# Big split products, term by term over the PSUM banks

## The chip, the cores and the metric

The kernel runs on one core of a Trainium2 chip. The metric is the device time of one execution in microseconds. A time is the median of several runs; beside it stands one execution recorded by the profiler, whose span is a little shorter than the runs' time.

## The reference, cut to what matters

One layer of a hybrid backbone: four token mixers (convolution module, mLSTM, gated DeltaNet, RWKV-7) on one combined input projection of 512 tokens (256 context, 256 latent), a gated merge, an output projection, and a gated ConvFFN on the 256 latent tokens.

```python
D_MODEL, SEQ, CTX_LEN, D_FF = 2048, 256, 256, 5632
sc, sx = split_cols(hc @ p['w_in']), split_cols(hx @ p['w_in'])      # all branches' columns
...                                                                  # scans of the branches
br = jnp.einsum('btnw,nwd->btnd', ys, w_br)
gates = jax.nn.sigmoid(gate_cols.reshape(*gate_cols.shape[:2], N_BRANCH, -1))
mx = jnp.sum(gates * br, axis=2) @ w_out
x = x + gt1x * rms_norm(mx, norm_g[l, 1])
...
u, v = jnp.split(h @ up, 2, axis=-1)
fx = (jax.nn.gelu(dwconv2d_grid(u, dw), approximate=True) * v) @ down
x = x + gt2x * rms_norm(fx, norm_g[l, 3])
```

Everything is float32.

## The kernel before, in words

**Split products.** A float32 product is made of three products in the faster fp32r type. Each operand is split in two parts: hi is the value rounded to fp32r, lo is what is left. The sum of hi·hi, hi·lo and lo·hi is the product. The activations' parts are `uh` and `ul` (in the FFN `u2h`, `u2l`, and `hh`, `hl` for the down product); a weight tile's parts are `hi` and `lo`. So each pair of a weight tile and an activation tile costs three matmuls, here called terms; one of the three needs the weight's `lo`.

**The weight stream.** A step handles 256 rows of a weight matrix, that is two K tiles of 128, for up to 512 columns. `load_split` (line 181) issues the DMA from SyncE into `raw`, lets ScalarE copy it into `hi` (line 192) and VectorE, or at times GpSimdE, subtract `hi` from `raw` into `lo` (line 194). `raw` has four buffers (five in the FFN), `hi` and `lo` two each (four in the FFN). A buffer is used again when its last reader is done: `raw` after the `lo` split, `hi` and `lo` after the last matmul that reads them.

**mode_b** (line 201, with `mode_b_steps`) keeps the weights stationary: out[channel, token], one PSUM bank per block of 128 channels, and up to four blocks in a set. A set has `nkt/2` steps, eight for the 2048 rows. It is used for most columns of the input projection and for FFN up.

**mode_a** (line 220) keeps the activations stationary: out[token, channel], one bank per tile of 128 tokens, 512 channels. It is used for the branch gates (16 sets of eight steps), for the merge (`merge`, 16 sets of two steps), for mLSTM's v and for the output projection. With `apart`, the last so many steps of a set are held back and done token tile by token tile; the output projection's last set does that with three steps.

In both, a step goes bank by bank: all six matmuls of one bank (two K tiles, three terms), then the next bank. The second term of mode_a and the third of mode_b needs `lo`.

**FFN down** (in `ffn`, line 1407) has 44 steps, one per K tile of 128 rows, 24 matmuls each, into eight banks: two token tiles `i` by two halves `q` by two quarters `r`. `load_split_row` (line 1515; `hi` at 1523, `lo` at 1524) loads each half of a step. The last three steps are held and go bank by bank.

**What sets the order.** The program's text gives the order of priority; the framework's scheduler (`schedule_with_timeline_sim=True`) then writes each engine's queue with a simulated timeline, and may draw an instruction ahead of another that it takes to be late. Matmuls into the same bank stay in order. On the chip each engine works its queue from front to back. The sets of columns run beside the branches' scans, so split work and scan work share VectorE and ScalarE. All matmuls are recorded at line 79, the helper `mm`.

Of the kernel before, what the change touches and what calls it, by code (L numbers as in the profile page):

```python
# [20 lines left out]
P = 128  # L21
D = 2048
# [10 lines left out]
# columns of the per-channel parameters: first one, number  # L33
# [8 lines left out]
class Kern:  # L42
# [4 lines left out]
    # ---------------------------------------------------------------- helpers  # L47
# [13 lines left out]
    def aux(self, name="aux", tag="aux"):  # L61
        """PSUM bank; its tag's banks go round in program order."""
        bufs = self.auxn.get(tag)
        assert bufs, tag
        return self.auxp.tile([P, 512], F32, tag=tag, name=name, bufs=bufs)
# [8 lines left out]
    def evp(self, name):  # L74
        """PSUM behind column sets and adaLN, apart from the recurrences'."""
        return self.wap.tile([P, 512], F32, tag="wa", name=name)
# [4 lines left out]
    def tr(self, out, in_, b=0):  # L81
        """out = in_.T; in_ starts at partition b."""
        k = in_.shape[0]
        self.nc.tensor.transpose(out, in_, self.ident[b : b + k, b : b + k])
# [9 lines left out]
    def rsqrt(self, pool, x, shape, tag):  # L94
        """x ** -0.5 in place of a small fp32 tile of positive values (Newton from a bit-level guess)."""
# [6 lines left out]
        # y (15 - 10 a + 3 a^2) / 3 of a = x y^2, then y' (3 - 9/64 x y'^2) 3/16  # L102
# [9 lines left out]
    # ---------------------------------------------------------------- constants  # L112
    def constants(self):
# [15 lines left out]
        # LM[:, kind, col] over (row % 64): 0 col>row, 1 col>=row, 2 col<row, 3 col<=row  # L129
# [7 lines left out]
        # block-diagonal 128x128 versions  # L137
# [19 lines left out]
    def first_params(self):  # L157
        """Per-channel parameters, one column per 128 channels; c and c_ctx first."""
# [5 lines left out]
    def params(self):  # L164
        nc, PC = self.nc, self.PC
        # a = 1 - mu0 - mu1 of the token shift
# [10 lines left out]
    # ---------------------------------------------------------------- weight stream  # L177
# [3 lines left out]
    def load_split(self, parts, width, rings=None):  # L181
        """parts: [(dram [256, w], column offset)] -> hi, lo tiles [128, 2, 512] in fp32r."""
# [13 lines left out]

    def mode_b(self, *a):
        for _ in self.mode_b_steps(*a):
            pass

    def mode_b_steps(self, parts_of, width, blocks, uh, ul, nkt, bank=None):
        """Weights stationary: out[channel, token]. blocks: (offset, M, token0, N, evacuate).
        One step per pair of K tiles; the evacuations follow the last."""
        ps = [bank("psB") if bank else self.mmp.tile([P, 512], F32, tag="mm", name="psB") for _ in blocks]
        n2 = nkt // 2
        for kg in range(n2):
            hi, lo = self.load_split(parts_of(kg), width)
            for bi, (off, M, t0, N, _) in enumerate(blocks):
                for k in range(2):
                    kt = 2 * kg + k  # L210
                    for j, (w, u) in enumerate(((hi, uh), (hi, ul), (lo, uh))):
                        self.mm(ps[bi][:M, :N], w[:, k, off : off + M], u[:, kt, t0 : t0 + N],
                                start=(kt == 0 and j == 0), stop=(kt == nkt - 1 and j == 2))
# [6 lines left out]
    def mode_a(self, parts_of, uh, ul, nkt, toks, evac, apart=0, rings=None):  # L220
        """Activations stationary: out[token, channel] for 512 channels. apart: this many last steps go by token tile."""
# [3 lines left out]
        for kg in range(n2):  # L225
            hl = self.load_split(parts_of(kg), 512, rings if kg % 2 else None)
            todo = [(kg, hl, ti) for ti in range(len(toks))]
            if kg >= n2 - apart:
                held.append(todo)
                todo = [t[ti] for ti in range(len(toks)) for t in held] if kg == n2 - 1 else []  # L230
            for g, (hi, lo), ti in todo:
                t0 = toks[ti]
                for k in range(2):
                    kt = 2 * g + k
                    for j, (u, w) in enumerate(((uh, hi), (uh, lo), (ul, hi))):
                        self.mm(ps[ti], u[:, kt, t0 : t0 + P], w[:, k, :],
                                start=(kt == 0 and j == 0), stop=(kt == nkt - 1 and j == 2))
# [3 lines left out]
    # ---------------------------------------------------------------- adaLN  # L241
    def wmod_steps(self, cb, dst, raws=None, gain=None):
        """One step per 256 rows of w_mod[:, 512 cb:][:512]; the last one leaves silu(c) @ it + b_mod in dst, feature-major
        [128, 4, 1 or 2]. The partial sums of column half h lie on rows 64 h + 32 k + {0: c, 1: c_ctx}."""
# [18 lines left out]
        if gain is not None:  # L263
            # a gate vector on every partition, times the norm's gain
# [25 lines left out]
    def mod_feed(self):  # L290
        """Steps of the other four adaLN vectors of the latent stream, taken beside the column sets: shift and scale of the
        FFN feature-major, the gates token-major."""
# [6 lines left out]
    def feed(self, upto=0):  # L299
        """As many adaLN steps as the rate says, and all before step `upto`."""  # L300
# [5 lines left out]
    # ---------------------------------------------------------------- phase 0  # L306
    def phase0(self, first, opened):
        """adaLN shift and scale of the mixer, modulated input u (context tokens first); `first`: the steps of
        column sets that run as its K tiles appear; `opened`: called before their last ones."""
# [38 lines left out]
        # what is left of u takes the place of the token tiles  # L348
# [42 lines left out]
    # ---------------------------------------------------------------- inverse of unit triangular 64x64 blocks  # L391
# [7 lines left out]
    def tinv(self, pool, tag, d, n, N, U, pool_rec=False, ptag="aux"):  # L399
        """U[:, j] = (I - N[:, j])^-1 for n matrices per half of the partitions: rows s on partitions (two blocks  # L400
# [1268 lines left out]
```

## Time and profile before

| | us |
|---|---|
| median of 3 runs | 2360.63 |
| lowest, highest | 2359.28, 2361.23 |
| profiled execution, span | 2358.9 |
| TensorE matmuls busy | 2250.4 (95%) |
| VectorE busy | 1478.0 (63%) |
| ScalarE busy | 987.1 (42%) |
| GpSimdE busy | 500.8 (21%) |

The profiled execution's own time is known by its span alone. The rows name engines PE (TensorE matmuls), PEld (its weight loads), DVE (VectorE), ACT (ScalarE), POOL (GpSimdE) and SP (SyncE, which issues the DMAs). A row of a group gives busy time, the mean duration of one in ns, and the idle time of the engine ahead of it with what ended it. A row of the timeline gives start, duration, engine, line, operation, out<-in and, in brackets, the idle time ahead. Matmuls are pipelined: a row's duration overlaps the next, and the pace is the distance of starts. `psB`, `psA` and `psD` are the banks of mode_b, mode_a and FFN down. In rows of windows the columns are length, then busy time and count for PE, PEld, DVE, ACT and POOL, then the granted clock of TensorE, the DMA engines' busy share and GB/s.

In time, the input's modulation lies from 0 to 150 us, the column sets and the scans to about 900, the gates' sets with scans beside them to about 1400, the merge and output projection to about 1560, FFN up from 1575 to 2106, and FFN down to the end.

### The profile page before, as it was taken

The numbers are of one execution on the slowest core, as the hardware profiler recorded it, in microseconds if no ns is written. First come the engines' busy times: TensorE is split into PE (matmuls) and PEld (weight loads), VectorE is DVE, ScalarE is ACT, GpSimd is POOL, SyncE is SP. The second block draws the span as 40 slices with busy tenths as digits, with TensorE's granted clock in tenths as the row PEclk, the third lists the DMA queues.
The fourth block names the chain that finished last, engine by engine and source line by source line (L and its number), as shares of the span: only waits on it lengthen the run. The fifth ranks groups of instructions, "written<-read, shape, count | busy, mean of one in ns | idle before, by whom it ended". The sixth has DMA issues, their size and how long they took to land.

```text
span 2358.9 us, 42865 instructions
## 1 busy us (share of the span) xinstructions
PE 2250.4 (95%) x16820; PEld 1846.2 (78%) x16820; DVE 1478.0 (63%) x3079; ACT 987.1 (42%) x1491; POOL 500.8 (21%) x849
## 2 busy tenths in 40 slices
PE   6979899999999899999999999989999999999998
PEld 3657677877888666767777777779999999998886
DVE  3357866643555976566556478566777677775554
ACT  4225644433444343233225544444444344444443
POOL 0012563533452995000001034010000000000000
PEclk8989899899999999999999999989999999999999
DMA  9934654454666677677668667567767666666563
GB/s 367 347 113 129 180 166 117 133 169 135 184 180 197 184 239 216 208 238 233 189 206 275 185 223 262 184 224 216 225 210 218 208 182 187 180 199 204 193 195 101
DMA packets 273612, 471.97 MB, mean 200 GB/s; under 512 B 41505, under 2 KB 80673, under 8 KB 272417
## 3 DMA queue, kind: packets, MB, share of 16 engines
q1 hardware_dynamic: 273122, 467.14, 63.6%
q8 instruction: 132, 2.16, 0.4%
q10 hardware_dynamic: 288, 2.10, 0.2%
q14 instruction: 70, 0.57, 0.1%
HBM read 440.33 MB, written 28.84 MB: 199 GB/s over the span
## 4 chain that ended last, share of the span: by engine, by line
PE 80%; DVE 8%; DMA 5%; ACT 2%; POOL 2%; issue 2%; SPq 0%; DVEq 0%; ACTq 0%; POOLq 0%
PE psB L79 35%; PE psA L79 20%; PE psD L79 10%; PE psw L79 4%; DVE lo L194 2%; DMA wraw<-in_w_mod 2%; PE psG L79 1%; DMA raw<-in_w_mix 1%; DVE cacc L858 1%; POOL riU L397 1%; PE pVN L79 1%; PE pKS L79 1%; PE pSn L79 1%; ACT hi L192 1%; PE psf L79 1%
## 5 line engine op out<-in xcount | busy, mean ns | idle before, releaser
L194 DVE TENSOR_TENSOR lo<-raw,hi 128x1024 fp32r<-128x1024 f32 (+2 forms) x485 | 603.6, 1246 | 449.7 <-ACT hi L192 440.2
L192 ACT ACTIVATE hi<-raw 128x1024 fp32r<-128x1024 f32 (+2 forms) x488 | 508.4, 1043 | 845.4 <-PE psB L79 383.7
L79 PE MATMUL psB<-u2h,lo 128*128 128x256 f32 x1408 | 396.7, 283 | 0.0
L79 PE MATMUL psB<-u2l,hi 128*128 128x256 f32 x1408 | 396.5, 283 | 0.2 <-DVE u2l L1354 0.2
L79 PE MATMUL psB<-u2h,hi 128*128 128x256 f32 x1408 | 395.5, 285 | 1.1 <-DVE u2h L1353 1.1
L79 PE MATMUL psA<-lo,uh 128*128 128x512 f32 x832 | 336.3, 405 | 12.6 <-DVE lo L194 12.3
L79 PE MATMUL psA<-hi,ul 128*128 128x512 f32 x832 | 329.8, 397 | 0.0
L79 PE MATMUL psA<-hi,uh 128*128 128x512 f32 x832 | 310.0, 404 | 2.2 <-ACT hi L192 2.2
L79 PE MATMUL psB<-uh,hi 128*128 128x256 f32 (+1 forms) x832 | 281.5, 347 | 24.4 <-ACT hi L192 17.8
L79 PE MATMUL psB<-ul,hi 128*128 128x256 f32 (+2 forms) x832 | 278.9, 340 | 0.0
L79 PEld LDWEIGHTS psB<-u2h,hi 128*128 128x128 f32 x1408 | 267.6, 192 | 10.8 <-issue 9.5
L79 PEld LDWEIGHTS psB<-u2l,hi 128*128 128x128 f32 x1408 | 269.9, 192 | 0.5 <-DVE u2l L1354 0.5
L79 PEld LDWEIGHTS psB<-u2h,lo 128*128 128x128 f32 x1408 | 269.8, 192 | 0.1
L79 PE MATMUL psB<-uh,lo 128*128 128x256 f32 (+2 forms) x832 | 263.1, 342 | 6.8 <-DVE lo L194 6.8
L79 PEld LDWEIGHTS psA<-lo,uh 128*128 128x128 f32 x832 | 156.9, 189 | 63.0 <-DVE lo L194 21.7
L79 PEld LDWEIGHTS psB<-uh,hi 128*128 128x128 f32 x832 | 159.9, 193 | 54.8 <-ACT hi L192 20.7
L79 PEld LDWEIGHTS psA<-hi,uh 128*128 128x128 f32 x832 | 153.5, 189 | 51.5 <-issue 15.0
L79 PEld LDWEIGHTS psA<-hi,ul 128*128 128x128 f32 x832 | 157.0, 189 | 33.6 <-issue 1.0
L79 PEld LDWEIGHTS psB<-uh,lo 128*128 128x128 f32 (+1 forms) x832 | 153.8, 192 | 32.3 <-DVE lo L194 9.6
L79 PEld LDWEIGHTS psB<-ul,hi 128*128 128x128 f32 (+1 forms) x832 | 160.6, 193 | 22.0 <-issue 6.1
L1524 DVE TENSOR_TENSOR lo<-raw,hi 128x1024 fp32r<-128x1024 f32 x88 | 107.6, 1225 | 78.3 <-ACT hi L1523 78.2
L1444 DVE SCALAR_TENSOR_TENSOR facc<-fpad,ffdw,facc 128x256 f32<-128x256 f32 x352 | 152.9, 488 | 0.2
(569 smaller groups left out, 3129.1 us busy)
## 6 DMA issues: line engine op xcount, KB each, us to landing
raw<-in_w_in SPq DMA_DIRECT2D x208, 512.0 KB, 4.5
raw<-in_ffn_up SPq DMA_DIRECT2D x176, 512.0 KB, 3.9
wraw<-in_w_mod SPq DMA_DIRECT2D x160, 512.0 KB, 5.3
raw<-in_ffn_down SPq DMA_DIRECT2D x88, 512.0 KB, 4.6
raw<-in_w_br SPq DMA_DIRECT2D x32, 512.0 KB, 4.8
raw<-in_w_out SPq DMA_DIRECT2D x32, 512.0 KB, 4.7
raw<-in_w_mod SPq DMA_DIRECT2D x32, 512.0 KB, 4.0
raw<-in_w_in SPq DMA_DIRECT2D x48, 256.0 KB, 3.7
```

Source lines behind the costliest of these rows:

```text
L79: self.nc.tensor.matmul(out, lhsT, rhs, start=start, stop=stop)
L192: nc.scalar.activation(hi[s], raw[s], AF.Copy)
L194: (nc.gpsimd if self.pool_lo >= 0 else nc.vector).tensor_tensor(lo[s], raw[s], hi[s].bitcast(F32), ALU.subtract)
L397: eng.tensor_tensor(U16[:, :, t], U16[:, :, t], m[:, :, t], ALU.add)
L858: nc.vector.scalar_tensor_tensor(a, cpad[:, i, t : t + 256], w(i, t), a, ALU.mult, ALU.add)
L1444: nc.vector.scalar_tensor_tensor(s3(acc), pad[:, dy : dy + 4, dx : dx + 64], tap(t, b), s3(acc), ALU.mult, ALU.add)
L1524: nc.vector.tensor_tensor(f(lo), f(raw), f(hi).bitcast(F32), ALU.subtract)
```

## The change

A new helper gives the order of a step's matmuls, as (bank, K tile, term). In the middle steps of a set, all but the first and the last, it goes term by term: for each term both K tiles, and for each of these all banks. In other steps it stays bank by bank. In mode_a the terms change places, so that the one with `lo` is the last everywhere; in mode_b it was the last already. Steps that `apart` holds back count as last ones, so they stay bank by bank. FFN down goes term by term over all eight banks in its first 41 steps, and bank by bank in the three held ones, with the term of `lo` last in both. The sets of the merge have two steps, so there only the order of terms changes. The numbers of instructions, tiles and buffers stay.

```diff
+    def turns(n, by_term):
+        if by_term:
+            return [(b, k, j) for j in range(3) for k in range(2) for b in range(n)]
+        return [(b, k, j) for b in range(n) for k in range(2) for j in range(3)]
...
     def mode_b_steps(self, parts_of, width, blocks, uh, ul, nkt, bank=None):
...
-            for bi, (off, M, t0, N, _) in enumerate(blocks):
-                for k in range(2):
-                    kt = 2 * kg + k
-                    for j, (w, u) in enumerate(((hi, uh), (hi, ul), (lo, uh))):
-                        self.mm(ps[bi][:M, :N], w[:, k, off : off + M], u[:, kt, t0 : t0 + N],
-                                start=(kt == 0 and j == 0), stop=(kt == nkt - 1 and j == 2))
+            terms = (hi, uh), (hi, ul), (lo, uh)
+            for bi, k, j in self.turns(len(blocks), 0 < kg < n2 - 1):
+                (off, M, t0, N, _), (w, u), kt = blocks[bi], terms[j], 2 * kg + k
+                self.mm(ps[bi][:M, :N], w[:, k, off : off + M], u[:, kt, t0 : t0 + N],
+                        start=(kt == 0 and j == 0), stop=(kt == nkt - 1 and j == 2))
...
     def mode_a(self, parts_of, uh, ul, nkt, toks, evac, apart=0, rings=None):
...
-            todo = [(kg, hl, ti) for ti in range(len(toks))]
+            todo = [(kg, hl, t) for t in self.turns(len(toks), 0 < kg < n2 - max(apart, 1))]
             if kg >= n2 - apart:
                 held.append(todo)
-                todo = [t[ti] for ti in range(len(toks)) for t in held] if kg == n2 - 1 else []
-            for g, (hi, lo), ti in todo:
-                t0 = toks[ti]
-                for k in range(2):
-                    kt = 2 * g + k
-                    for j, (u, w) in enumerate(((uh, hi), (uh, lo), (ul, hi))):
-                        self.mm(ps[ti], u[:, kt, t0 : t0 + P], w[:, k, :],
-                                start=(kt == 0 and j == 0), stop=(kt == nkt - 1 and j == 2))
+                todo = [t for ti in range(len(toks)) for h in held for t in h if t[2][0] == ti] if kg == n2 - 1 else []
+            for g, (hi, lo), (ti, k, j) in todo:
+                (u, w), kt = ((uh, hi), (ul, hi), (uh, lo))[j], 2 * g + k
+                self.mm(ps[ti], u[:, kt, toks[ti] : toks[ti] + P], w[:, k, :],
+                        start=(kt == 0 and j == 0), stop=(kt == nkt - 1 and j == 2))
...
-            order = [(hh, hl, w, k, i, q) for q in range(2) for i in range(2)]
+            order = [(hh, hl, w, k, i, q, r, j) for j in range(3) for q in range(2) for i in range(2) for r in range(2)]
...
-                order = [t + (i, q) for i in range(2) for q in range(2) for t in held]
-            for uh, ul, w, kk, i, q in order:
+                order = [t + (i, q, r, j) for i in range(2) for q in range(2) for t in held for r in range(2) for j in range(3)]
+            for uh, ul, w, kk, i, q, r, j in order:
                 hi, lo = w[q]
-                for r in range(2):
-                    for j, (u, v) in enumerate(((uh, hi), (uh, lo), (ul, hi))):
-                        self.mm(ps[i][2 * q + r], u[:, P * i : P * i + P], v[:, r, :],
-                                start=(kk == 0 and j == 0), stop=(kk == 43 and j == 2))
+                u, v = ((uh, hi), (ul, hi), (uh, lo))[j]
+                self.mm(ps[i][2 * q + r], u[:, P * i : P * i + P], v[:, r, :],
+                        start=(kk == 0 and j == 0), stop=(kk == 43 and j == 2))
```

The rest of the diff takes out comments.

More of the change, by code (lines that the diff above doesn't have):

```diff
@@ L195, in load_split @@
         return hi, lo
+    @staticmethod
+    def turns(n, by_term):
+        if by_term:
+            return [(b, k, j) for j in range(3) for k in range(2) for b in range(n)]
+        return [(b, k, j) for b in range(n) for k in range(2) for j in range(3)]
     def mode_b(self, *a):
```

## The prediction

> **What bounds the kernel now.** I read the page first (engines, chain of waits), then the chain in order of time, then who TensorE waits for, and last the busy table of the stretches where those waits lie.
>
> ```profile
> span 2358.9 us, 42865 instructions
> PE 2250.4 (95%) x16820; PEld 1846.2 (78%) x16820; DVE 1478.0 (63%) x3079; ACT 987.1 (42%) x1491; POOL 500.8 (21%) x849
> ...
> PE 80%; DVE 8%; DMA 5%; ACT 2%; POOL 2%; issue 2%; SPq 0%; DVEq 0%; ACTq 0%; POOLq 0%
> ```
>
> TensorE is the bound: 95% busy and 80% of the chain. Idle time on it is 2358.9 - 2250.4 = 108.5 us, and an order of matmuls can only win from that, or from the pace of matmuls. First the pace, from the chain in order of time and the timeline of the down product:
>
> ```profile
> 1448.01 5.56 PE psA L79 x24
> ...
> 1606.68 11.70 PE psB L79 x96
> ...
> 1870.32 233.77 PE psB L79 x1948
> ```
>
> ```profile
> 2199.52 0.39 PE L79 MATMUL psD<-hi,hl 128*128 128x512 f32 x1
> 2199.75 0.39 PE L79 MATMUL psD<-hi,hh 128*128 128x512 f32 x1
> 2199.98 0.39 PE L79 MATMUL psD<-lo,hh 128*128 128x512 f32 x1
> 2200.20 0.39 PE L79 MATMUL psD<-hi,hl 128*128 128x512 f32 x1
> ```
>
> The piece at 1606.68 holds 96 matmuls of FFN up, four steps of 24: with the last one's 0.28 us off, 95 starts in 11.4 us, 0.120 us each. Within it the bank changes every six matmuls. In the down product the step from hi,hl to hi,hh is always a change of bank and takes 0.23 us, the other two steps stay in a bank and take 0.23 and 0.22. So a change of bank costs nothing here, and a chain of adds into one bank does not slow a matmul either. At 1870.32 stand 1948 matmuls of FFN up without a break. The FFN therefore has nothing to give from the order itself. A product with 512 columns goes at (5.56 - 0.39) / 23 = 0.225 us.
>
> Next, whom TensorE waits for; the columns are total us, times, longest:
>
> ```profile
> PE psA L79 <- DVE lo L194: 12.3, 16, 1.9
> PE psB L79 <- DVE lo L194: 6.8, 6, 1.4
> ...
> PE psD L79 <- DVE lo L1524: 0.7, 1, 0.7
> ```
>
> Waits for lo are 12.3 + 6.8 + 0.7 = 19.8 us, 0.84% of the span: all that this change can take away directly. Where they lie, by the same view cut to windows (200 to 312, 770 to 893, and 1405 to 1442, in that order):
>
> ```profile
> PE psB L79 <- DVE lo L194: 5.4, 4, 1.4
> ...
> PE psA L79 <- DVE lo L194: 9.4, 10, 1.9
> ...
> PE psB L79 <- DVE lo L194: 1.4, 2, 1.0
> ...
> PE psA L79 <- DVE lo L194: 2.2, 5, 0.7
> ```
>
> And how busy the engines are there (first PE, then DVE as the third, POOL as the fifth):
>
> ```profile
> 200.00:310.00 110.00, 97.46 (x472) 75.59 (x471) 84.36 (x112) 71.17 (x107) 52.81 (x41) 0.94 0.58 166
> 770.00:830.00 60.00, 51.30 (x375) 40.20 (x373) 58.30 (x87) 20.46 (x28) 57.89 (x52) 0.97 0.61 177
> ...
> 853.00:893.00 40.00, 33.28 (x291) 22.70 (x290) 38.94 (x120) 16.56 (x22) 39.45 (x40) 1.00 0.67 199
> 893.00:1000.00 107.00, 107.00 (x809) 77.86 (x808) 58.80 (x118) 35.21 (x45) 26.79 (x27) 0.98 0.74 222
> 1407.00:1442.00 35.00, 32.68 (x139) 24.40 (x137) 31.43 (x44) 12.77 (x16) 19.98 (x12) 1.00 0.83 285
> ```
>
> This is the reading that decides. Where the waits for lo are thickest, VectorE is 97% busy (58.30 of 60, 38.94 of 40), and 90% from 1407. There lo is late because VectorE is full, and a later place for the lo term does not make VectorE faster: in a stretch of several steps the wait moves along to the next step. Behind 893 TensorE has no idle time.
>
> **What the present order already does.** The queues are not in program order; around a late lo the trace shows other banks' hi terms drawn ahead:
>
> ```profile
> 215.73 0.68 PE L79 MATMUL psB<-uh,hi 128*128 128x256 f32 x1
> ...
> 216.25 0.28 PE L79 MATMUL psB<-ul,hi 128*128 128x256 f32 x1
> ...
> 216.97 0.28 PE L79 MATMUL psB<-ul,hi 128*128 128x256 f32 x1
> ...
> 217.29 1.22 DVE L194 TENSOR_TENSOR lo<-raw,hi 128x1024 fp32r<-128x1024 f32 x1
> ...
> 218.57 0.39 PE L79 MATMUL psB<-uh,lo 128*128 128x256 f32 x1 [1.32 <-DVE lo L194]
> ```
>
> From 215.73 to 216.97 lie eight hi matmuls, two for each of four banks, before the first lo. A bank's own sums stay in order, so mode_b has a cover of two matmuls per bank already, and mode_a, whose second term is lo, one. By term it is four per bank (two K tiles, two hi terms). The cover thus grows in mode_b with four blocks from 8 to 16 matmuls, 8 x 0.120 = 0.96 us; in mode_b with two blocks of 512 from 4 to 8, 4 x 0.225 = 0.9 us; in mode_a with two token tiles from 2 to 8, 6 x 0.225 = 1.35 us. In the merge (two steps a set, no middle one) and in first and last steps only the order of terms in mode_a changes, from 2 to 4: 0.45 us.
>
> **The change part by part.** No matmul, weight load, split or DMA is added or removed; SP and POOL queues are not passed by anything. Releases move: hi is free after two thirds of a step, lo at its very end.
>
> (a) 200 to 312, mode_b. Four waits, 5.4 us; each shrinks by at most some 0.95, together 3.8. In this stretch ACT and VectorE are busy 71 and 84 of 110 us with the RWKV features, and the chain goes through them as often as through TensorE, so I take half: -2.0 (ends: 0 and -5.4).
>
> (b) 770 to 893. Twelve waits, 10.8 us, VectorE full. What is left as gain is at the ends of the stretch. The rows around its first end:
>
> ```profile
> 825.25 0.79 PE L79 MATMUL psA<-lo,uh 128*128 128x512 f32 x1 [1.88 <-DVE lo L194]
> ...
> 825.84 0.63 PE L79 MATMUL psA<-hi,ul 128*128 128x512 f32 x1
> ...
> 826.26 0.63 PE L79 MATMUL psA<-hi,uh 128*128 128x512 f32 x1
> ...
> 829.47 1.06 ACT L192 ACTIVATE hi<-raw 128x1024 fp32r<-128x1024 f32 x1 [2.31 <-PE psA L79]
> ...
> 832.20 1.04 POOL L1097 TENSOR_TENSOR gKd<-gKd,erem 128x512 f32<-128x512 f32 x1 [1.51 <-ACT erem L1026]
> ```
>
> The lo wait holds back ten matmuls of that step, these hold back hi's release, and ACT's in-order queue with the split at 829.47 holds back the decays, for which POOL sits idle 1.51 us. With hi done before lo, that goes: -1.5. At the other end,
>
> ```profile
> 890.82 1.59 DVE lo L194
> 892.45 7.16 PE psA L79 x23
> ```
>
> behind the last late lo four matmuls remain in place of ten: -1.35. Together -2.9 (ends: 0 and -10.8).
>
> (c) 1405 to 1442, the merge: 2.2 us in five waits, each shrinking by at most 0.45, VectorE at 90%: -0.6 (ends 0 and -2.2).
>
> (d) The rest: in out_proj 12.3 - 9.4 - 2.2 = 0.7 in psA, of which 0.5 by the cover; and the start of the down product:
>
> ```profile
> 2107.38 0.73 PE L79 MATMUL psD<-hi,hh 128*128 128x512 f32 x2 [1.15 <-ACT hi L1523]
> 2108.77 0.79 PE L79 MATMUL psD<-lo,hh 128*128 128x512 f32 x1 [0.67 <-DVE lo L1524]
> ```
>
> There the new order takes the hi of the second half at the fifth matmul, not the thirteenth. ScalarE makes four of them in a row from 2106.27:
>
> ```profile
> 2106.27 3.90 ACT L1523 ACTIVATE hi<-raw 128x1024 fp32r<-128x1024 f32 x4 [1.89 <-PE psB L79]
> ```
>
> so the second is there at about 2106.27 + 2 x 0.98 = 2108.2, while four matmuls from 2107.38, at the slow pace of 0.42 us of 825.84 to 826.26 above, last to 2109.1. No new wait, and the lo wait goes: -0.7. Together -1.2 (ends 0 and -1.4). Middle steps of FFN up and down: 0, since no wait for lo stands in them.
>
> Sum: -2.0 - 2.9 - 0.6 - 1.2 = -6.7 us against the profiled 2358.9, whose span is 1.7 below the median of the runs (2360.63). I forecast 2360.6 - 6.7 = 2354; its own range is 2349 to 2358.
>
> **A rule beside the rows.** Matmuls behind the wait at 825.25 start 0.42 us apart in place of 0.225: a wait of 1.88 us also brings a slow spell. The Trainium skill, "TensorE: Matmul & The Clock Gate", section Part 1: The HAM clock gate, says that the clock is halved after an idle activity window of about 3.4 us and given back after a busy one. The halved pace agrees; a wait of 1.88 us alone is shorter than its window, so by that rule this spell need not come again or vanish with the wait. The sum stands without it.
>
> **The rivals.** R1: the waits for lo are only a symptom, and all of (a) to (c) move along: VectorE ends its lo at the same times, and TensorE waits for the last four matmuls in place of the last ten, while POOL finds another late input. Only (d) is left: 2359.4. For it: VectorE at 97%. Against it: 893 to 1000 has no idle time on TensorE, so what is done earlier there counts in full.
>
> R2: every lo wait goes, -19.8, and the slow spell with it, 7 x 0.2 = 1.4: 2339.4. For it: the longest wait is 1.9 us and most are under the added cover. Against: VectorE's share.
>
> R3, the other side: VectorE gets blocked. Its queue works in order, and a lo split needs the buffer of the lo two steps back. That buffer is now free one matmul later (0.225 us), and hi, which the split waits for, comes up to four matmuls earlier, so the buffer can become the last thing waited for. Two full stretches hold 28 and 11 splits:
>
> ```profile
> L194 DVE TENSOR_TENSOR lo<-raw,hi 128x1024 fp32r<-128x1024 f32 x28 | 38.8, 1386 | 7.6 <-ACT hi L192 7.6
> ...
> L194 DVE TENSOR_TENSOR lo<-raw,hi 128x1024 fp32r<-128x1024 f32 x11 | 15.4, 1397 | 2.8 <-ACT hi L192 2.7
> ```
>
> If each is held by 0.225 us, 39 x 0.225 = 8.8 us: 2369.4. It decides from 21 such holds on (4.7 us). Against it: all idle time before these splits is ended by ACT's hi, none by TensorE. A new order of the queues that puts a split ahead of a recurrence's small work would look the same and cost as much.
> The Trainium skill, "PSUM — Partial Sum Buffer", section Engine vs sequencer instructions, calls the queues of ScalarE, VectorE and GpSimdE strict FIFO, which is what R3 needs; the split at 829.47 holding the decays agrees.
>
> **How the numbers follow.** A measurement of this kernel can tell about 0.2%, 4.7 us, from no change: faster is below 2355.9, slower above 2365.3. Chances: forecast 0.42, R1 0.25, R2 0.14, R3 0.19. Of the forecast's range 2349 to 2358 some 0.85 lies below 2355.9: faster 0.36 + 0.14 = 0.50; the same 0.06 + 0.25, with a little of R3, 0.32; slower 0.18. The range 2343 to 2367 leaves out about half of R2 and half of R3, 0.17.
>
> **What would show it.** Right: waits of psA for lo fall from 12.3 to below 8 us, their number falls, the wait for lo in psD is gone, FFN up stays at 0.120 us a matmul, POOL's gKd wait at about 832 shrinks. R1: lo waits as many, further back in a step. R2: hardly any, and PE idle below 90 us. R3: VectorE waiting for TensorE ahead of lo, or longer gaps between the delta rule's small matmuls. I am wrong from the ground up if a matmul's pace changes with the bank at every matmul: 0.005 us on the 3 x 1408 of FFN up, one of whose three groups is
>
> ```profile
> L79 PE MATMUL psB<-u2h,hi 128*128 128x256 f32 x1408 | 395.5, 285 | 1.1 <-DVE u2h L1353 1.1
> ```
>
> would be 21 us.

## The result, and the profile after

The change makes the kernel slower. Four runs of it have a median of 2375.26 us (2373.89 to 2381.27), four runs of the kernel before 2359.95 us: a ratio of 1.0066, 95% interval 1.0051 to 1.0082, some 15 us. The forecast was 2354, the range ended at 2367. The profiled execution took 2374.77 us, its span is 2373.1, 14.2 us more than before.

The first lines of the page of the changed kernel:

```profile
span 2373.1 us, 42836 instructions
PE 2249.4 (95%) x16820; PEld 1848.0 (78%) x16820; DVE 1466.7 (62%) x3079; ACT 981.1 (41%) x1487; POOL 512.9 (22%) x849
```

TensorE's busy time is unchanged (2250.4 before). So all of the loss is idle time on TensorE: 2373.1 - 2249.4 = 123.7 us in place of 108.5. Here are the waits of TensorE in the changed kernel (total us, times, longest):

```profile
PE psB L79 <- ACT hi L192: 23.3, 4, 12.9
PE psho L84 <- DVE mlh L797: 7.1, 1, 7.1
PE psA L79 <- DVE lo L194: 6.7, 11, 1.4
PE psB L79 <- DVE lo L194: 4.5, 4, 1.6
PE psn L79 <- ACT mA L1246: 4.4, 3, 1.7
...
PE psD L79 <- ACT hi L1526: 2.1, 1, 2.1
...
PE psD L79 <- DVE lo L1527: 0.6, 1, 0.6
```

The same view of the kernel before, for the one row that the prediction did not show:

```profile
PE psB L79 <- ACT hi L192: 17.8, 4, 13.3
```

The change did what it says: waits for lo fell from 19.8 us to 6.7 + 4.5 + 0.6 = 11.8. What came instead are 5.5 us more for hi in mode_b, 7.1 us for mLSTM's output (`mlh`) ahead of the transposes `psho`, and 4.4 us in mLSTM's scan (`psn`); the last two were not there at all.

How far such rows can be trusted is seen in two runs described below, `d_only` and `nodep_before`. Ahead of FFN down TensorE works through the same matmuls in the same order as in the kernel before, by names and shapes. Yet their waits for hi in psB are 14.9 and 17.9 us (before 17.8), for lo in psB 9.7 and 8.6 (6.8), for lo in psA 13.5 and 13.2 (12.3). A difference of 3 us in one such row between two profiles therefore shows nothing; TensorE's idle time in the stretches of the table below differs between these three by 1.2 us at most.

The pace held. The timeline of the changed kernel in FFN up and in the down product, by term:

```profile
2099.10 1.12 PE L79 MATMUL psB<-u2h,hi 128*128 128x256 f32 x8
2100.06 1.12 PE L79 MATMUL psB<-u2l,hi 128*128 128x256 f32 x8
2101.02 1.12 PE L79 MATMUL psB<-u2h,lo 128*128 128x256 f32 x8
...
2200.34 1.98 PE L79 MATMUL psD<-hi,hh 128*128 128x512 f32 x8
2202.15 1.98 PE L79 MATMUL psD<-hi,hl 128*128 128x512 f32 x8
```

Each matmul goes to another bank than the one before it: eight take 0.96 us, 0.120 each, and with 512 columns 1.81 us, 0.226 each. That is the pace of before.

**Where TensorE stands idle.** Busy time of TensorE in two stretches that cut the span where FFN up begins (the first two rows are before, at 1570, the other two after, at 1583; the first fence is of the kernel before):

```profile
0.00:1570.00 1570.00, 1474.02 (x11283) 0.97 0.65 203
1570.00:2359.00 789.00, 776.41 (x5539) 0.99 0.62 194
```

```profile
0.00:1583.00 1583.00, 1473.43 (x11282) 0.97 0.65 202
1583.00:2374.00 791.00, 775.97 (x5540) 0.99 0.62 193
```

Ahead of FFN up 96.0 us are idle before and 109.6 after: 13.6 of the 15.2 us. The FFN adds the other 1.6, of which 1.0 is the wait for hi at the start of the down product (1.1 before and 2.1 after).

Cut finer, at the first and last matmuls of the scans (before at 330.2, 756.3, 934.8, 1222.0, 1421.3, 1570.3 and 2107.4; after at 336.0, 755.1, 961.2, 1271.9, 1450.0, 1583.3 and 2121.5), TensorE's idle time is:

| stretch | before, us | after, us |
|---|---|---|
| up to RWKV's first step (`psR`) | 53.6 | 58.3 |
| RWKV's scan | 8.4 | 11.9 |
| from there to the delta rule's first step | 17.6 | 17.9 |
| the delta rule's recurrence | 3.4 | 2.8 |
| from its last step to mLSTM's output (`psho`) | 2.5 | 13.5 |
| from there to FFN up | 10.5 | 5.1 |
| FFN up | 2.4 | 4.1 |
| FFN down and the end | 10.0 | 10.0 |

The largest entry is the one around mLSTM's end: 11.0 us more, of which 7.1 are the wait for `mlh`.

**The order of TensorE's queue.** The delta rule's recurrence has 16 steps; its matmuls `pVN` from first to last, in the kernel before and then in the changed one:

```profile
L79 PE MATMUL pVN<-gX,gU x128: 269/269/320, 934.8 to 1222.0; 64*64 64x128 f32 x128
```

```profile
L79 PE MATMUL pVN<-gX,gU x128: 269/269/320, 961.2 to 1271.9; 64*64 64x128 f32 x128
```

It ends 50 us later. How many matmuls of the gates' sets (`psA`) run ahead of its first step, between first and last, and from there to mLSTM's `psho` is in the windows cut at these times, with those matmuls alone; before, then after:

```profile
0.00:934.80 934.80, 150.45 (x574) 0.96 0.62 191
934.80:1222.40 287.60, 193.47 (x771) 1.00 0.70 214
1222.40:1421.20 198.80, 154.98 (x624) 1.00 0.73 230
```

```profile
0.00:961.20 961.20, 169.77 (x670) 0.96 0.61 190
961.20:1272.20 311.00, 214.19 (x867) 1.00 0.73 216
1272.20:1450.00 177.80, 118.81 (x480) 0.97 0.71 227
```

A matmul that lies across a cut is counted on both sides, so a sum of these rows is one too high. Ahead of the last step of the delta rule stand 192 more gate matmuls (1536 against 1344). The 96 more between first and last step account for the longer recurrence: 96 x 0.23 = 22 us, and 311.0 - 287.6 = 23.4 us, while TensorE is no more idle there (2.8 us, before 3.4). No work is added by that. But there are only 2016 such matmuls that do not need mLSTM's result: 16 gate sets of 96, 192 for v, three merges of 96. After the change all 2016 have run when mLSTM's output is due: the reserve is used up. Before, 1968 had run, and 48 were left. What TensorE then does, in the timeline of the changed kernel:

```profile
1442.49 0.39 PE L79 MATMUL psA<-lo,uh 128*128 128x512 f32 x1
1449.99 1.54 PE L84 MATMUL psho<-ident,mlh 128*128 128x128 f32 x6 [7.11 <-DVE mlh L797]
```

Nothing is left to run beside mLSTM's end; before, `psho` came at 1421.32 in the middle of gate and merge matmuls, with no wait.

**A second place, early.** ScalarE's timeline, of the kernel before and then of the changed one:

```profile
213.28 0.63 ACT L608 ACTIVATE rfE<-rfc 128x512 f32<-128x512 f32 x1
...
214.08 1.04 ACT L192 ACTIVATE hi<-raw 128x1024 fp32r<-128x1024 f32 x1
...
215.85 1.04 ACT L192 ACTIVATE hi<-raw 128x1024 fp32r<-128x1024 f32 x1
...
219.88 0.60 ACT L599 ACTIVATE rfsg<-pslo 128x512 f32<-128x512 f32 x1 [1.08 <-DVE rfAR L612]
```

```profile
215.77 0.63 ACT L612 ACTIVATE rfE<-rfc 128x512 f32<-128x512 f32 x1
...
221.72 1.28 ACT L603 ACT_TABLE_LOAD   x1 [1.08 <-DVE rfAR L616]
223.02 0.60 ACT L603 ACTIVATE rfsg<-pslo 128x512 f32<-128x512 f32 x1
223.51 0.59 ACT L603 ACTIVATE rfic<-pslo 128x512 f32<-128x512 f32 x1
223.99 2.00 ACT L192 ACTIVATE hi<-raw 128x1024 fp32r<-128x1024 f32 x2
```

Before, two splits stand right behind the first decay features. After the change they stand behind the next pair's features, which wait for VectorE. TensorE pays for it (changed kernel):

```profile
225.10 2.08 PE L79 MATMUL psB<-uh,hi 128*128 128x256 f32 x8 [6.11 <-ACT hi L192]
```

### The profile page after: what moved, and what is told of

Read it like the earlier page. It is cut to its first block, busy times and chain, and to the rows that moved or that the text cites. A ratio compares the mean times of both kernels' runs of the same rounds, so it can differ in the third digit from the quotient of the medians.

```text
span 2373.1 us, 42836 instructions
## 1 busy us (share of the span) xinstructions
PE 2249.4 (95%) x16820; PEld 1848.0 (78%) x16820; DVE 1466.7 (62%) x3079; ACT 981.1 (41%) x1487; POOL 512.9 (22%) x849
## 4 chain that ended last, share of the span: by engine, by line
PE 57%; DVE 3%; DMA 1%; ACT 0%; POOL 0%; issue 0%; DVEq 0%; SPq 0%; ACTq 0%; POOLq 0%
PE psB L79 21%; PE psA L79 19%; PE psD L79 10%; PE psw L79 2%; DMA wraw<-in_w_mod 1%; PE pVN L79 1%; PE pKS L79 1%; DVE lo L194 1%; PE pSn L79 1%; PE psn L79 1%; PE psr L79 0%; PE pQS L79 0%; PE pO L79 0%; PE psq L79 0%; PE psf L79 0%; DVE gim L400 0%
## 5 line engine op out<-in xcount | busy, mean ns | idle before, releaser
L79 PE MATMUL psA<-lo,uh 128*128 128x512 f32 x832 | 264.3, 400 | 6.7 <-DVE lo L194 6.7
L79 PE MATMUL psB<-u2h,lo 128*128 128x256 f32 x1408 | 251.7, 284 | 0.0
L79 PE MATMUL psB<-u2h,hi 128*128 128x256 f32 x1408 | 250.1, 285 | 1.2 <-DVE u2h L1357 1.2
L79 PE MATMUL psB<-u2l,hi 128*128 128x256 f32 x1408 | 248.7, 283 | 0.8 <-DVE u2l L1358 0.8
L79 PE MATMUL psB<-uh,hi 128*128 128x256 f32 (+2 forms) x832 | 205.9, 350 | 26.3 <-ACT hi L192 23.3
L79 PEld LDWEIGHTS psB<-u2h,hi 128*128 128x128 f32 x1408 | 203.6, 192 | 10.5 <-ACT hi L192 4.5
L79 PEld LDWEIGHTS psB<-u2h,lo 128*128 128x128 f32 x1408 | 204.9, 192 | 0.5 <-issue 0.4
L79 PEld LDWEIGHTS psB<-u2l,hi 128*128 128x128 f32 x1408 | 204.2, 192 | 1.0 <-DVE u2l L1358 1.0
L79 PE MATMUL psB<-ul,hi 128*128 128x256 f32 (+2 forms) x832 | 198.9, 339 | 0.0
L79 PEld LDWEIGHTS psA<-lo,uh 128*128 128x128 f32 x832 | 154.2, 188 | 55.5 <-DVE lo L194 11.8
L79 PEld LDWEIGHTS psB<-uh,hi 128*128 128x128 f32 (+1 forms) x832 | 140.0, 195 | 58.2 <-ACT hi L192 26.3
```

The costliest lines, as they stand in the source:

```text
L79: self.nc.tensor.matmul(out, lhsT, rhs, start=start, stop=stop)
```

## The experiments

**Theory F** (for filler, the work that TensorE has to do while a scan waits): the new order of matmuls makes the scheduler write other queues, in which column and gate matmuls and feature work go ahead of the branches' recurrences and of splits; the recurrences end late, and TensorE stands bare behind mLSTM. Rivals: E puts the loss on mode_b's part in the early stages, G on mode_a's order by term itself; R3 is the prediction's, VectorE held by lo's buffer. Each kernel was timed in three rounds beside the kernel before. The edits are shown in part: those of `a_terms` and `a_banks` against `a_only`, those of the feed against the kernel named, that of `lo_third` against the whole change.

**The parts alone.** `a_only` has mode_a's part of the change and nothing else, `b_only` mode_b's, `d_only` FFN down's. `a_terms` is mode_a bank by bank in all steps, with lo last:

```diff
-            todo = [(kg, hl, t) for t in self.turns(len(toks), 0 < kg < n2 - max(apart, 1))]
+            todo = [(kg, hl, t) for t in self.turns(len(toks), False)]
```

> Only mode_a is changed (by term in middle steps, lo last); mode_b and FFN down as before. Theory F (filler first): with lo last the planner finds more matmuls of the gates' sets ready and puts them into TensorE's queue ahead of the delta rule and mLSTM scans. This queue has 1493 psA matmuls ahead of the last pVN, 149 more than before, at 0.231 us each: the last pVN starts about 34 us later than 1222 us, the gates end earlier, the filler is used up (2016 psA matmuls) before the last psho, and TensorE idles there. Time 2366 to 2372. Theory E (early loss): the 15 us come from mode_b in the first 520 us and are only carried along: then this kernel is at 2356 to 2361.

> Only mode_b is changed (by term in middle steps). Theory F: 36 more psA matmuls ahead of the last pVN than before, so the scan some 8 us later, 10 matmuls of filler left at the last psho: tail nearly covered, 2361 to 2367, with what the first 520 us lose. Theory E: the whole loss is here, 2372 to 2377. FFN up stays at 0.120 us a matmul under both.

> Only FFN down goes by term. Its TensorE queue up to the FFN is that of before. Both theories: 2359 to 2361, the wait for lo at the start of FFN down (0.67 us) gone or replaced by a wait for hi of about the same length; if bank changes at every matmul cost anything, 41 x 24 matmuls would show it as a pace above 0.227 us.

> mode_a stays bank by bank, but its term with lo is the last of three, not the second; all else as before. Theory F: 1427 psA matmuls ahead of the last pVN, 83 more than before: the last pVN about 19 us later, filler used up at the last psho, 2362 to 2368, between before and the kernel with all of mode_a changed. Theory E: 2357 to 2361.

| | us | before | ratio, 95% interval |
|---|---|---|---|
| a_only | 2369.39 | 2360.34 | 1.0044, 1.0031 to 1.0057 |
| b_only | 2367.15 | 2360.34 | 1.0031, 1.0019 to 1.0042 |
| d_only | 2360.75 | 2360.34 | 1.0002, 0.9991 to 1.0014 |
| a_terms | 2357.24 | 2360.34 | 0.9991, 0.9976 to 1.0005 |

FFN down is neutral. mode_a's part costs 0.44%, within F's forecast; mode_b's costs 0.31%, just above F's and well below E's. So E falls. The waits of TensorE in `a_only`:

```profile
PE psho L84 <- DVE mlh L796: 9.1, 1, 9.1
...
PE psA L79 <- DVE lo L194: 6.1, 9, 1.3
```

Its waits for lo in psA are half of before's 12.3, and it is 9 us slower: the bare tail outweighs them. `a_terms` is a miss for F. Its wait for `mlh` is 7.0 us, its recurrence ends 18 us late, and yet it is not slower. Its waits for lo in psA went from 12.3 to 7.0 us; those in psB (hi 14.9, lo 9.6) are what `d_only` has with the old order. TensorE's idle time is 2357.0 - 2248.6 = 108.4 us, as before. A bare tail alone does not decide; its sum with the other waits does.

**The order by term without the new place of lo.** `a_banks` is mode_a by term in the middle steps, lo second as before:

```diff
-                (u, w), kt = ((uh, hi), (ul, hi), (uh, lo))[j], 2 * g + k
+                (u, w), kt = ((uh, hi), (uh, lo), (ul, hi))[j], 2 * g + k
```

> mode_a term by term over the banks in middle steps, but with the lo term second as before. It has the same change of bank at every matmul as the kernel with mode_a alone, while the planner finds no more matmuls ready ahead of lo than before: 1360 psA matmuls ahead of the last pVN (1344 before, 1493 there), 1982 ahead of the last psho (1982, 2016). Theory F: 2357 to 2363. Theory G, order of banks: 2367 to 2372.

Measured 2359.37 against 2362.36, 0.9989 (0.9979 to 1.0). G falls: 512-column matmuls of mode_a that change the bank every time cost nothing. Since `a_only` differs from `a_banks` in the place of lo alone, its loss comes with that place. In the rows of `a_banks`,

```profile
PE psA L79 <- DVE lo L194: 16.7, 21, 1.9
```

the waits for lo are 4 us above before's (3 above those of `d_only`) and the time is not longer. Waits for lo were not what set the end.

**A slower feed of adaLN work**, meant to leave filler for the tail. `rate45` is the kernel before, `a_rate45` `a_only`, `terms_rate45` `a_terms`, each with

```diff
-        self.rate = 0.55
+        self.rate = 0.45
```

> mode_a changed as in the kernel with mode_a alone (2369.4), and the rate of adaLN steps among the columns 0.45 in place of 0.55, so that these come later and filler is left for the end of mLSTM: 1896 psA matmuls ahead of the last psho in place of 2016, that is 120 x 0.23 = 27 us of work still to do there. The delta rule stays as late (1528 psA matmuls ahead of the last pVN, 1493 there). Theory F (scans late, filler used up, tail bare): the wait of 9.1 us at psho goes, 2358 to 2363, with the last pVN still 35 us or more later than before. Theory G (going term by term is itself dearer, by the order of banks or the earlier release of hi): stays at 2367 to 2372.

> The kernel before with the adaLN rate 0.45 alone, a control for the run above. Theory F: before has hardly any bare tail (1.1 us idle between 1430 and 1525), so there is nothing to win: 2356 to 2362. If the rate has a worth of its own, apart from the tail: below 2354.

> mode_a bank by bank with lo last (2357.2 in its own run, with a wait of 7.0 us at psho) and the adaLN rate 0.45: 1816 psA matmuls ahead of the last psho in place of 2016. Theory F: that wait goes too, 2349 to 2354. Otherwise 2355 to 2361.

`a_rate45` took 2388.90 us, `rate45` 2393.39 and `terms_rate45` 2385.89, against 2362.36 (1.0111, 1.0130, 1.0097). As a test of the tail they failed: the merges cannot begin until all adaLN steps are fed, so the control itself lost 31 us. Waits of `rate45`:

```profile
PE psw L79 <- DMA wraw<-in_w_mod: 44.5, 17, 11.6
```

15 us more than in the kernel before (29.5), and TensorE is busy 105.6 of the 130 us from 1300 on, before 128.7. One thing can be read: with this feed the order by term in mode_a is 4.5 us, and lo last bank by bank 7.5 us, faster than the control, by medians of four runs. The order by term, which loses at one feed, gains at the other.

**The tail taken away.** In the merge the second branch (n = 1) reads branch 0's features, so that it does not depend on mLSTM; its result is another one. Done to before, to `a_only` and to the whole change (`nodep_before`, `nodep_a`, `nodep_after`):

```diff
+            m = 0 if n == 1 else n
-            self.mode_a(lambda kg: [...], self.uh[:, 4 * n : 4 * n + 4],
-                        self.ul[:, 4 * n : 4 * n + 4], 4, [0, P], ev)
+            self.mode_a(lambda kg: [...], self.uh[:, 4 * m : 4 * m + 4],
+                        self.ul[:, 4 * m : 4 * m + 4], 4, [0, P], ev)
```

> The kernel before, but the merge of the mLSTM branch reads the convolution branch's features in place of mLSTM's, so that no product waits for the end of mLSTM (the output is another; all instructions stay, 16820 matmuls). Before has 1.1 us idle between 1430 and 1525, so Theory F gives hardly a gain: 2355 to 2361. Theory G: the same.

> The kernel with mode_a alone changed (2369.4, 9 above before), with the same cut: the mLSTM branch's merge reads the convolution branch's features. Up to the merge TensorE's queue is that of mode_a alone, so the scans are as late (last pVN near 1264). Theory F: the late scan costs only through the bare tail at psho (9.1 us) and what else waits there, so the loss goes: 2356 to 2362, within 3 us of the kernel before with the same cut. Theory G (the loss lies in going term by term, all along): 2366 to 2371.

> The whole change, and in the merge the second branch (n = 1) reads branch 0's features in place of mLSTM's, so that its result isn't the layer's. Theory F (the change lets column and gate matmuls go ahead of the scans; the scans end late, and TensorE stands bare behind mLSTM's tail): what mode_a loses in that tail, 9 us less the 3 us that stayed in nodep_a, goes away, and mode_b's part stays; 2366 to 2371 us where before is 2361, and no wait for mlh ahead of psho. Rival (the loss lies along the scans themselves, not behind them): 2373 to 2378 as in the whole change.

`nodep_before` 2360.90 against 2361.20 (0.9999): taking the dependence away gains nothing where no tail is bare. `nodep_a` 2364.04 (1.0016, 1.0007 to 1.0025) in place of 1.0044: by the medians about two thirds of mode_a's loss was the tail. That lies between F's forecast (2356 to 2362) and G's (2366 to 2371): F expected nearly the whole loss to go. `nodep_after` 2368.51 against 2360.72 (1.0039, 1.0025 to 1.0052) in place of 1.0066: 0.27% of the whole change's 0.66%, some 6.5 us, near the 7.1 of the wait, which is gone. The recurrence ends as late as in the whole change (`nodep_after`):

```profile
L79 PE MATMUL pVN<-gX,gU x128: 269/269/320, 962.6 to 1272.7; 64*64 64x128 f32 x128
```

So what the wait for mLSTM costs goes, though the recurrence ends as late. 0.39% stays. In the stretches of the table above, cut the same way, this kernel is idle 57.1 us up to RWKV's first step, 11.9 in RWKV's scan and 6.6 between the delta rule's last step and `psho`, that is 3.5, 3.5 and 4.1 more than before; of the 6.6 us 4.4 are the waits in mLSTM's scan (`psn`). Whether these last ones come from the late recurrence too is not shown.

**mode_b by place.** `b_cols` is mode_b by term in the input projection's columns alone, `b_ffn` in FFN up alone, by a flag that is set ahead of each stage (the rest of the edit is mode_b's of the change):

```diff
+            for bi, k, j in self.turns(len(blocks), self.by_term and 0 < kg < n2 - 1):
```

> mode_b term by term only in the columns of the input projection (phase 0 included); FFN up, FFN down and mode_a as before. Theory F for mode_b: the column matmuls drawn ahead delay the adaLN products in phase 0 by some 4 us and the RWKV features by 5, of which 2 to 3 us are left at the start of the FFN: 2361 to 2365, more than half of the 7 us of mode_b alone. Rival (the loss lies in FFN up and its end): 2358 to 2361.

> mode_b term by term only in FFN up. Theory F: no scan runs beside it, so only the wait for hi at the start of FFN down may grow (1.15 us before, 2.8 with mode_b alone): 2359 to 2363. Rival: most of the 7 us of mode_b alone, 2364 to 2368.

2363.35 and 2363.79 against 2361.20: 1.0012 each (1.0002 to 1.0021 and to 1.0022). The early wait for hi is in every profile with mode_b by term in the columns. In TensorE's timeline of `b_cols`:

```profile
225.63 1.65 PE L79 MATMUL psB<-uh,hi 128*128 128x256 f32 x6 [6.12 <-ACT hi L192]
```

In the whole change it is 6.11 (4.29 in `lo_third`), and no profile with bank by bank there has it. `b_cols` is not 6 us slower, though: RWKV's scan (`psSA`) begins 6.3 us later than before, and ends 3.7 us later; part of the delay is taken up. In FFN up the pace is the same; what `b_ffn` loses is seen at the seam, in its timeline, the down product's first matmuls:

```profile
2113.05 0.73 PE L79 MATMUL psD<-hi,hh 128*128 128x512 f32 x2 [1.98 <-ACT hi L1529]
2114.89 0.79 PE L79 MATMUL psD<-lo,hh 128*128 128x512 f32 x1 [1.11 <-DVE lo L1530]
2115.48 0.63 PE L79 MATMUL psD<-hi,hl 128*128 128x512 f32 x1
2115.91 0.63 PE L79 MATMUL psD<-lo,hh 128*128 128x512 f32 x1
```

Waits of 1.98 + 1.11 us stand where before has 1.15 + 0.67, and the slow pace of 0.43 us behind them lasts to 2121, some 8 us; before it lasts from 2107 to 2112. The time lies between F's forecast for `b_ffn` (2359 to 2363) and the rival's (2364 to 2368).

**The whole change in variants.** `lo_second` has mode_a's terms as in `a_banks`. `after_late` and `lo2_late` are the whole change and `lo_second` with mode_b bank by bank in the first stage (to about 150 us), `lo2_nob` is `lo_second` with mode_b bank by bank everywhere; by the flag above.

> The whole change, but mode_a keeps the old order of its terms: lo second, by term over the banks. Theory F: in TensorE's queue 1392 psA matmuls stand ahead of the last delta-rule step (before 1344, the whole change 1536), so mode_a's loss goes and mode_b's and FFN down's stay, 5.9 + 0.4 us with mode_a's -2.7: 2362 to 2368 us where before is 2361, psA waits for lo back at 12 us or more. Rival (mode_a's order by term costs, together with mode_b's): 2372 to 2377.

> The whole change, but mode_b stays bank by bank in the first stage (RWKV's k columns, up to about 150 us). Theory: the adaLN products and the last quarter of u that come 5 us late there are carried to the end, so about 5 us come back: 2368 to 2372 us where before is 2361. Rival (TensorE's other work takes the gap up, the loss stays at the scans): 2374 to 2377. TensorE's queue behind that stage is the same as in the whole change.

> As lo_second (whole change, in mode_a lo second), and mode_b bank by bank in the first stage. If lo_second's loss lies in the first stage: 2361 to 2366 us where before is 2361; if it lies in the columns and gates' queue behind it: 2372 to 2376.

> As lo_second, with mode_b bank by bank everywhere: what is left of the change is mode_a by term with lo second, and FFN down by term. If mode_b is what lo_second lost by, the two neutral parts add to nothing: 2357 to 2362 us where before is 2361. If mode_a and FFN down add up to a loss that neither has alone: 2365 or more.

| | us | before | ratio, 95% interval |
|---|---|---|---|
| lo_second | 2375.32 | 2360.72 | 1.0056, 1.0041 to 1.0071 |
| after_late | 2373.64 | 2360.96 | 1.0053, 1.0036 to 1.0071 |
| lo2_late | 2371.12 | 2360.96 | 1.0037, 1.0026 to 1.0048 |
| lo2_nob | 2360.73 | 2360.96 | 1.0001, 0.9991 to 1.0010 |

`lo_second` is a plain miss for F, and its time is the rival's (2372 to 2377). The tail is all but filled (`psho` waits 2.0 us), the recurrence ends 31 us earlier than in the whole change, and the time is the same. `lo2_nob` shows which part does it: without mode_b's part nothing is lost. So by the medians mode_b by term costs 0.31% beside the old mode_a and 0.55% beside mode_a by term; the parts do not simply add. Where `lo_second` stands idle, by TensorE's windows of before and then of `lo_second`:

```profile
170.00:310.00 140.00, 123.42 (x598) 0.92 0.53 152
...
830.00:1300.00 470.00, 458.10 (x3263) 1.00 0.74 226
```

```profile
170.00:310.00 140.00, 116.19 (x568) 0.90 0.50 146
...
830.00:1300.00 470.00, 452.72 (x3230) 0.99 0.71 218
```

7 us more are idle in the stretch with the early wait for hi; counted from the start to RWKV's first step it is 59.1 against 53.6, 5.5 more. In the second stretch it is 5 us more, but in the delta rule's recurrence itself only 0.7 (4.1 against 3.4); the rest lies ahead of it and behind it. Leaving out the first stage gains 0.13% (`after_late`) and 0.19% (`lo2_late`) by the medians, but the intervals overlap each time, so that it gains anything is not shown. Both times lie between the two forecasts made for them. In the first stage, in TensorE's timeline of `b_only`, adaLN's next products stand behind 12 hi matmuls of a set, and these run at half pace behind a wait:

```profile
106.98 1.08 PE L79 MATMUL psw<-wraw,cst 128*32 128x256 f32 x8 [2.00 <-DMA wraw<-in_w_mod]
108.00 5.40 PE L79 MATMUL psB<-uh,hi 128*128 128x512 f32 x12
```

Why mode_b by term costs more in `lo_second` than in `b_only` is not settled.

**R3 by itself.** In the whole change VectorE waits for TensorE ahead of lo, as R3 has it; before there is no such row. VectorE's waits of the changed kernel:

```profile
DVE lo L194 <- PE psB L79: 40.0, 19, 9.3
...
DVE lo L194 <- PE psA L79: 18.3, 12, 3.2
```

`lo_third` gives the whole change a third lo buffer:

```diff
-        self.rawp = self.pool("rawp", bufs=4, stack=ses)
+        self.rawp = self.pool("rawp", bufs=3, stack=ses)
-        self.lop = self.pool("lop", bufs=2, stack=ses)
+        self.lop = self.pool("lop", bufs=3, stack=ses)
```

> The whole change with three lo buffers in place of two in all stages before the FFN; to make room raw has three in place of four. VectorE's waits for TensorE ahead of lo (32, 59.1 us in the whole change, none before) should be gone or nearly. R3 (VectorE held by the lo buffer makes the scans late): last pVN back by 20 us or more, to below 1250, no wait for mlh ahead of psho, 2358 to 2366 us where before is 2361, unless the missing raw buffer shows as TensorE waiting for hi. F (the order of TensorE's queue makes them late): the queue has 1584 psA matmuls ahead of the last delta-rule step, as many as in the whole change (1536) or more, so last pVN stays at 1265 to 1285, the wait for mlh stays, and 2371 us or more.

Measured 2385.39 against 2361.71 (1.0096, 1.0079 to 1.0113). VectorE's and TensorE's waits in `lo_third`, and the recurrence:

```profile
DVE lo L194 <- PE psB L79: 2.0, 1, 2.0
...
PE psho L84 <- DVE mlh L797: 7.5, 1, 7.5
...
L79 PE MATMUL pVN<-gX,gU x128: 269/269/320, 972.4 to 1289.4; 64*64 64x128 f32 x128
```

With VectorE's waits gone the recurrence still takes 317 us and ends late, and the wait for `mlh` stays, as F has it. The run does not hold the order fixed, though: TensorE's queue was written anew, with 1584 `psA` matmuls ahead of the last step, 48 more than in the whole change. What the missing raw buffer adds to the time is not told apart either. Two other runs help: VectorE waits ahead of lo for psB 41.4 us in `b_only` and 40.8 us in `lo_second`, as long as in the whole change, and their recurrences end at 1234.8 and 1241.0. So these holds alone do not make a recurrence as late as 1271.9.

What does go with the late end is the number of `psA` matmuls ahead of the last step: 1344 and an end at 1222.0 before, 1360 and 1228.7 in `a_banks`, 1380 and 1234.8 in `b_only`, 1392 and 1241.0 in `lo_second`, 1427 and 1240.0 in `a_terms`, 1493 and 1264.5 in `a_only`, 1536 and 1271.9 in the whole change, 1584 and 1289.4 in `lo_third`. From the first to the last of these each one more goes with about 0.28 us, of which 0.23 is the matmul itself.

## Why the prediction was wrong

- **The pace (middle steps 0).** Right: 0.120 and 0.226 us with a change of bank at every matmul; `a_banks` and `d_only` are neutral. FFN up by term is not quite nothing, 0.12% in `b_ffn`, but at its seam with FFN down.
- **Waits for lo.** Right as a count (psA from 12.3 to 6.7 us, forecast below 8), and wrong as a price. The prediction took every us of lo wait that goes for a us of time. `a_only` loses 9 us with 6.1 us of such waits, `a_banks` none with 16.7. TensorE works through one order of a fixed amount of work; an earlier matmul is worth something only where the whole reserve is not about to run out later.
- **(a) -2.0.** Wrong in sign. In this stretch the psB waits for lo fell from 5.4 to 1.6, the whole 3.8 that stood there before it was halved, but the step assumed that the queues of ScalarE stay as they were. They were written anew, two splits went behind the next pair's features, and 6.1 us of waiting came in.
- **(b) -2.9.** Between RWKV's scan and the delta rule the waits for lo shrank from 10.8 to 9.2 us, and their number went from 12 to 13. Nothing was won by it (idle time there 17.6 before, 17.9 after), as R1 had it for this step. The argument made against R1 failed, that TensorE has no idle time behind 893, so that "what is done earlier there counts in full": this is the step on which the sum rests. What was done earlier were gate matmuls, 96 of them ahead of the recurrence and 96 more inside it. GpSimdE's `gKd` no longer waits, as forecast, but it runs at 852 in place of 832.
- **(c) -0.6.** The merge's waits for lo went; in their place stands the bare 7.1 us. From `psho` to FFN up 5.4 us less are idle, and ahead of it 11.0 us more. This step was costed by the merge's own waits and not by what has to be left over to fill mLSTM's end.
- **(d) -1.2.** With FFN down alone by term (`d_only`) the psD wait for lo fell from 0.7 to 0.2 us and that for hi stayed 1.1, as the step had it, but a wait of 1.0 for `h` came in: "no new wait" failed, and the time shows no gain (1.0002). In the whole change the wait for lo fell to 0.6 only and that for hi rose by 1.0. The rise goes with FFN up by term, which the step did not count: in `b_ffn`, with the old FFN down, the wait for hi is 2.0, and in `lo2_nob`, with the old FFN up, 1.1.
- **R3.** The right sign, but its mechanism does not carry the loss: the holds are there (31 of them, 58 us, 29 us of it in the first 200 us), and the recurrence is late without them in `lo_third` and not nearly as late with the psB ones in `b_only`. Its last sentence, a new order of the queues that looks the same, is what happened, other way round: small work and filler ahead of splits and recurrences. It was not given a price of its own. The row for it was there: 1344 of the 2016 free matmuls gone by the end of the recurrence, and only 48 left (2016 - 1968) when `psho` came.
- **The slow spell.** It did not go: behind short waits matmuls still start 0.43 us apart, in the whole change from 2124.22 to 2126.78, and in the rows of `b_ffn` (2115.48 to 2115.91).

What is shown: the loss is idle time; 0.27% of 0.66% is the bare end of mLSTM (`nodep_after`), FFN down nothing. Only located, by the table of stretches, and not taken away one by one: 4.7 us more up to RWKV's first step, 3.5 in RWKV's scan, 3.9 in mLSTM's scan beside the 7.1 of its end, 1.7 in FFN up, against 5.4 less from `psho` to FFN up. The delta rule's stretch has no part in it. Open: what each of these is worth by itself, the first stage above all; why the parts do not add; and why the scheduler takes the recurrences to be later, since its simulated timeline is not on record.

## What to carry to other kernels

Where a scheduler writes the queues, an edit of a big product's order is also an edit of everything beside it: count, ahead of each recurrence's steps, how much filler stands before and after, and how much is left when the last recurrence ends. A wait on the busiest engine is worth its length only if the work that moves up is not needed as cover later. Try each part of a change alone and then together: here the parts were 0.44, 0.31 and 0.02%, the whole 0.66%, and a variant without the place of lo that made mode_a's loss still lost 0.56%.

## What was not expected of the hardware

A change of PSUM bank at every matmul has no price that these runs show: eight matmuls of 512 columns go to eight banks in 1.81 us. Short waits can cost more than their length: behind waits of 1.98 and 1.11 us (`b_ffn`, 2113 to 2115) matmuls start 0.43 us apart in place of 0.226, at a granted clock of 0.50 (2116 to 2120). In `b_only` 12 matmuls behind waits of 0.50, 0.75 and 2.00 us take 5.40 us in place of 2.9, at a granted clock of 0.50 (107 to 110). Not every such wait does it: in the kernel before, behind one of 1.95 us at 819.55, matmuls start 0.23 us apart, while behind one of 1.88 us at 825.25 they start 0.42 us apart. The Trainium skill, "TensorE: Matmul & The Clock Gate", section Part 1: The HAM clock gate, lets the clock be halved after an idle window of about 3.4 us; in these rows no single wait ahead of the half pace is that long. ScalarE's change of function showed as a load of 1.28 us in its queue (221.72), a length that every reordering of its work moves about.
